# Rotary embedding and attention scores on one core: loads that follow a store issued as 64-row halves, with four loads through GpSimd in place of five

## The chip, the core and the metric

The kernel runs on one core of a Trainium2 chip. Its engines are TensorE (PE, matrix products; its weight loads are shown apart as PEld), VectorE (DVE), ScalarE (ACT), GpSimd (POOL) and SyncE (SP). Work of different engines is ordered by semaphores. Data moves between the core's on-chip memory (SBUF, 128 partitions) and the device's memory through 16 DMA engines. SyncE and GpSimd issue these transfers on rings of their own, and a transfer that an engine issues is spread over several or all of the 16. TensorE writes its results to PSUM, from where ScalarE or VectorE copies them to SBUF.

The metric is the time of one execution in device microseconds (us). Smaller is better.

## What is computed

Queries and keys get a rotary embedding, then each query row is multiplied with all key rows of its batch and head:

```python
batch, seq, heads, dim = 16, 512, 16, 64
q1, q2 = q[..., :half_dim], q[..., half_dim:]
q_rot = concatenate([q1 * cos - q2 * sin, q1 * sin + q2 * cos], axis=-1)
# k_rot the same from k
scores = einsum('bshd,bthd->bsht', q_rot, k_rot)
```

All is float32. The inputs q and k have 33.6 MB each, the output 16 x 512 x 16 x 512 values or 268.4 MB. The output is by far the most of the traffic.

## The kernel before

**Tiles and steps.** A batch has 512 rows. They are laid out so that SBUF partition p holds rows 4p to 4p+3; such a quarter, 128 rows with one of the four offsets, is a chunk (C = 4 chunks a batch). The kernel makes 64 steps, one for each chunk of q (`i` from 0 to 63, batch `i // 4`). In a step, TensorE forms the scores of 128 query rows against all 512 key rows, two heads at a time (`scores(i, p)` for p from 0 to 7), ScalarE copies each pair of heads from PSUM to the staging tile (line 418), and after the last pair the staging tile, 128 x 8192 values or 4 MB, is stored with one DMA (line 426). There are three staging tiles (`st`), used in turn; a tile may be filled again when its store has landed. The first batch is done in another order and stores 16 pieces of 1 MB.

**Preparing the chunks.** VectorE applies the rotary embedding in place (line 335), TensorE transposes the chunk through a small PSUM bank (line 360), and VectorE or ScalarE copies it to `qT` or `kT` (line 378). Within a step, the next chunk of q and a chunk of the next batch's k are prepared between the score products.

**Loads.** A batch of q or of k is 2 MB, 16 KB on each of the 128 partitions, and is loaded whole into one of two buffers for each of q and k (`load`, line 264). In the third step of a batch q of the batch after next is loaded, in the fourth step k of the batch after that (lines 507 to 510). SyncE issues them in the same ring as the stores, in the order in which the program's list has them: the store of the step, then the load.

**Loads around one DMA engine.** The kernel takes it that DMA engine 4 works more slowly than the other 15 (`SLOW = 4`). Five loads of q, those of batches 5, 8, 11, 13 and 15 (`RELIEVED`, line 260), are therefore split. [...] 

**Waits.** `Plan.add` records every operation with the keys that it reads and writes, and `Plan.resolve` works out from the keys which semaphore each has to await. A DMA names its own semaphore, for example `out0` for the first staging tile. A load's two groups of keys, `rows` and `rest`, let its two parts be awaited together where they come by different transfers. Line numbers of DMAs in the profile are those of the helper that records them (line 237).

Of the kernel before, what the change touches and what calls it, by code (L numbers as in the profile page):

```python
# [7 lines left out]
PE, ACT, DVE, POOL, SP = "PE", "ACT", "DVE", "POOL", "SP"  # L8
# [170 lines left out]
def kernel(  # L179
# [8 lines left out]
    nc = tc.nc  # L188
# [4 lines left out]
    B, S, H, D = q.shape  # L193
    HD = D // 2
    P = 128
    C = S // P
    HP = H // 2
# [8 lines left out]
    dram = {  # L206
        "q": q.rearrange("b (p c) h d -> b p c h d", c=C),
        "k": k.rearrange("b (p c) h d -> b p c h d", c=C),
    }
    o_v = out.rearrange("b (p c) h t -> b c p h t", c=C)  # L210
# [18 lines left out]
    def one(f):  # L229
        def emit():  # L230
            a = f()
            return a, a

        return emit

    def dma(engine, e, dst, src, sem, reads=(), writes=(), also=()):
        plan.add(engine, one(lambda: e.dma_start(dst, src)), reads, writes, sem=sem, also=also)  # L237
# [19 lines left out]
            writes=[("unit", which, u) for u in us], also=[x for u in us for x in unit_keys(which, u)],  # L257
        )

    RELIEVED = {("q", 5): 0, ("q", 8): 1, ("q", 11): 2, ("q", 13): 3, ("q", 15): 4}  # L260
    tiny = [0]
    SLOW = 4

    def load(which, b):
        if b >= B:
            return
        t = inb[which][b % 2]
        sem = f"in_{which}{b % 2}"
        rows = [("in", which, b % 2, c) for c in range(C)]
        rest = [("in rest", which, b % 2, c) for c in range(C)]  # L270
        if (which, b) not in RELIEVED:
            dma(SP, nc.sync, t.rearrange("p c (h d) -> p c h d", h=H), dram[which][b], sem, writes=rows + rest)
            return

        n, E, F = 120, C * H * D, C * H * D // 2
        x = RELIEVED[which, b]
        d = dram[which][b]  # L280

        def move_cursor(k):
            y = tiny[0]
            tiny[0] += 1
            src = bass.AP(q.tensor, 512 * y, [(512, k), (64, 2), (1, 2)])
            dst = scratch[:k, 4 * y : 4 * y + 4].rearrange("p (a b) -> p a b", a=2)
            dma(POOL, nc.gpsimd, dst, src, "cursor", writes=[("scratch", y)])

        def halves(lo, hi, keys, sem):
            src = bass.AP(d.tensor, d.offset + lo * E + F, [(E, hi - lo), (-F, 2), (1, F)])  # L290
            v = t[lo:hi]
            dst = bass.AP(v.tensor, v.offset + F, [(v.ap[0][0], hi - lo), (-F, 2), (1, F)])
            dma(POOL, nc.gpsimd, dst, src, sem, writes=keys)

        plan.add(POOL, None, (), rows)
        if x % 2:
            move_cursor(8)
            halves(n, P, rest, f"rest{x}")
        move_cursor(SLOW + 1)
        halves(0, n, rows, f"part{x}")  # L300
        if not x % 2:
            dma(SP, nc.sync, t[n:].rearrange("p c (h d) -> p c h d", h=H), d[n:], sem, writes=rest)
# [9 lines left out]
    def rope(which, n):  # L312
        if n < C:
            x = units[which, n]
            sv, k1, k2 = "p c (g j) -> p c g j", {"j": HD}, {"j": D}
            cs = cos_t.unsqueeze(2).to_broadcast((P, C, 2 * G, HD))
            ss = ss_v.unsqueeze(2).to_broadcast((P, C, G, D))
            pv = part.rearrange("p (c g j) -> p c g j", c=C, j=D)
            x5 = x.rearrange("p c (h x j) -> p c h x j", x=2, j=HD)
            p5 = part.rearrange("p (c h x j) -> p c h x j", c=C, x=2, j=HD)  # L320
            adds = [(x5[:, :, :, y], p5[:, :, :, 1 - y]) for y in range(2)]
        else:
            x = inb[which][n // C % 2][:, n % C]
            sv, k1, k2 = "p (g j) -> p g j", {"j": HD}, {"j": D}
            cs = cos_t[:, n % C].unsqueeze(1).to_broadcast((P, 2 * H, HD))
            ss = ss_v[:, n % C].unsqueeze(1).to_broadcast((P, H, D))
            pv = part.rearrange(sv, **k2)
            x4 = x.rearrange("p (h x j) -> p h x j", x=2, j=HD)
            swapped = bass.AP(part.tensor, part.offset + HD, [part.ap[0], (D, H), (-HD, 2), (1, HD)])
            adds = [(x4, swapped)]  # L330
        xs, xc = x.rearrange(sv, **k2), x.rearrange(sv, **k1)
        keys, more = src_keys(which, n), src_also(which, n)

        def tt(o, a, b, op, reads, writes):
            plan.add(DVE, one(lambda: nc.vector.tensor_tensor(o, a, b, op=op)), reads, writes, also=more)  # L335

        def products():
            tt(pv, xs, ss, mult, keys + ["ss"], ["part"])
            tt(xc, xc, cs, mult, keys + ["cos"], keys)

        def sums():
            for y, z in adds:
                tt(y, y, z, add, keys + ["part"], keys)

        return [products, sums]
# [34 lines left out]
    def stage_of(i):  # L380
        return i % 2 if i < C else (i - 2) % NST_BUFS
# [4 lines left out]
    def ps_of(i, p):  # L386
        m = HP * i + p if i < FIRST else HP * ((i - FIRST) % PERIOD) + p
        if i >= FIRST and m >= HP * PERIOD - 3:
            return (1, 2, 1)[m - (HP * PERIOD - 3)]
        return m % NPS  # L390

    def scores(i, p):
        y, s = ps_of(i, p), stage_of(i)
        ps, st = ps_s[y], stage[s]
        b = i // C
        if b == 0:
            c, hp = divmod(p, 2)
            lhs, rhs = qTb[i % 2][:, C * hp + c], kTb[0][:, 2 * i + hp]
            keys = [("qT", i % 2, C * hp + c)] + [("kT", 0, 2 * i + hp, x) for x in range(C)]
        else:  # L400
            lhs, rhs = qTb[i % 2][:, p], kTb[b % 2][:, p]
            keys = [("qT", i % 2, p)] + [("kT", b % 2, p, x) for x in range(C)]

        def emit():
            done = []
            for r in range(2):
                lo, hi = 64 * r, 64 * r + 64
                done.append(
                    nc.tensor.matmul(out=ps[:, r, :], lhsT=lhs[lo:hi, :], rhs=rhs[lo:hi, :], start=True, stop=True)  # L409
                )  # L410
            return done[0], done[-1]

        plan.add(PE, emit, keys, [("ps", y)])
        so, si = st[:, 2 * p : 2 * p + 2, :], ps
        if b > 0:
            so = so.rearrange("s r (t c) -> s r t c", c=C)
            si = si.rearrange("s r (c t) -> s r t c", c=C)
        plan.add(ACT, one(lambda: nc.scalar.copy(out=so, in_=si)), [("ps", y)], [("st", s, p)])  # L418
        if b == 0 and p % 2 == 1:
            c = p // 2  # L420
            dma(
                SP, nc.sync, o_v[0, c, :, G * i : G * (i + 1)], st[:, G * c : G * (c + 1)], f"out{s}_{c}",
                reads=[("st", s, p - 1), ("st", s, p)],
            )
        elif b > 0 and p == HP - 1:
            dma(SP, nc.sync, o_v[b, i % C], st, f"out{s}", reads=[("st", s, x) for x in range(HP)])

    def tr_act(which, n):
        for g in range(2):
# [2 lines left out]
    def run(ops):  # L432
        for op in ops:
            op()
# [3 lines left out]
    for head, heads in ((0, G), (G, H - G)):  # L438
        load_units("k", head, heads)
        load_units("q", head, heads)  # L440
    load("k", 1)
    load("q", 1)
    plan.add(POOL, one(lambda: nc.gpsimd.memset(ident, 0.0)), (), ["ident"])
    plan.add(
# [3 lines left out]
                out=ident, in_=ident, compare_op=mybir.AluOpType.not_equal, fill=1.0, base=0,  # L448
# [11 lines left out]
    for i in range(C):  # L460
        plan.step = i
        if i < C - 1:
            dve = rope("k", i + 1) + rope("q", i + 1) + rope("k", C + i)
            nxt = [("k", i + 1), ("q", i + 1)]
        else:
            dve = rope("q", C) + rope("k", C + i) + rope("q", C + 1) + rope("k", 2 * C)
            nxt = [("q", C), ("k", C + i)]
# [16 lines left out]
    for i in range(C, NST):  # L484
        plan.step = i
        tr = {}
        if i + 1 < NST:
            tr[1], tr[3] = ("q", i + 1, 0), ("q", i + 1, 1)
        if i + C < NST:
            tr[5], tr[6] = ("k", i + C, 0), ("k", i + C, 1)  # L490
        dve = []
        if i + 2 < NST:
            dve += rope("q", i + 2)
        if i + 1 + C < NST:
            dve += rope("k", i + 1 + C)
        for p in range(HP):
            scores(i, p)
            if p not in tr:
                continue
            if tr[p][0] == "q":  # L500
                run(dve[:1])
                dve = dve[1:]
                transposed(*tr[p], DVE)
            else:
                transposed(*tr[p], ACT)
        run(dve)
        if i % C == C - 2:
            load("q", i // C + 2)
        elif i % C == C - 1:
            load("k", i // C + 3)  # L510

    plan.resolve()
    with tc.tile_critical(), nc.cleanup_on_exit():
# [33 lines left out]
```

## Time and profile before

| | |
|---|---|
| Median of 3 runs | 797.21 us (795.77 to 797.94) |
| The profiled execution: its time | 797.94 us |
| its span in the profile | 796.2 us |
| PE matmuls, busy | 683.7 us (86%) |
| ACT, busy | 562.4 us (71%) |
| DVE, busy | 545.2 us (68%) |
| POOL, busy | 9.8 us (1%) |
| Moved by DMA | 335.87 MB, 422 GB/s over the span |
| Read from and written to device memory | 67.24 MB and 268.44 MB |

The page gives each engine's busy time, then a table in which the span is cut into 40 equal slices: a digit is the busy share of a slice in tenths, and the row GB/s says what the DMA engines moved. Below it stand the DMA queues, the chain of work that ended last, the costliest groups of instructions with the idle time before them, and the DMA issues with the median time from issue to landing. Two more views are used: the waits (who waited for whom: total, times, longest), and stretches of the span with the busy time of each engine (PE, PEld, DVE, ACT, POOL, each with its number of instructions), the clock granted to TensorE, the DMA engines' share and their rate. The trace also keeps a record of every DMA packet (start, duration, size, ring) and of every step by which a transfer counted up its semaphore, one for each DMA engine that took part.

### The profile page before, as it was taken

To read this page: it belongs to the slowest core of one execution; us is meant where nothing else is said; L and a number is where in the kernel's file an instruction comes from. 1 tells how busy PE (TensorE), PEld (TensorE's weight loads), DVE (VectorE), ACT (ScalarE), POOL (GpSimd) and SP (SyncE) were. 2 spreads that over 40 slices of the span, in tenths; PEclk is the share of its full clock that TensorE was granted. 3 is DMA by queue.
4 is the path that set the end of the run, shared out by engine and by line. 5 is a ranking of instruction groups with operands and counts; after the bars stand their busy time and mean duration, and the time that the engine had idled before them with its cause. 6 is when DMAs were issued, how large, how long until landed. Compare 5 with 4: busy or idle time off the path is not lost.

```text
span 796.2 us, 8200 instructions
## 1 busy us (share of the span) xinstructions
PE 683.7 (86%) x3072; PEld 294.7 (37%) x3072; DVE 545.2 (68%) x516; ACT 562.4 (71%) x647; POOL 9.8 (1%) x20
## 2 busy tenths in 40 slices
PE   3989999896998979899797988979978899799960
PEld 2444444342433434334342433334433344344420
DVE  6999988585785868658586767667756678576400
ACT  2978887684866858578585866767857777589760
POOL 0000000000000000100000000000100000000000
PEclk9999999897998989989899999999999999899995
DMA  8999999999999999999999999999999999999996
GB/s 347 419 425 437 423 394 435 425 436 423 435 417 428 435 433 424 433 424 411 432 426 439 430 433 427 429 424 428 435 428 419 421 440 427 429 433 431 434 430 278
DMA packets 18689, 335.87 MB, mean 422 GB/s; under 512 B 2184, under 2 KB 3464, under 8 KB 4488
## 3 DMA queue, kind: packets, MB, share of 16 engines
q1 hardware_dynamic: 16704, 325.46, 96.1%
q0 software_dynamic: 1680, 10.10, 3.0%
q10 hardware_dynamic: 288, 0.13, 0.1%
q8 instruction: 6, 0.10, 0.0%
q14 instruction: 11, 0.09, 0.0%
HBM read 67.24 MB, written 268.44 MB: 422 GB/s over the span
## 4 chain that ended last, share of the span: by engine, by line
DMA 47%; PE 35%; DVE 8%; ACT 6%; issue 1%; ACTq 0%; DVEq 0%; SPq 0%
DMA out_dram<-st 47%; PE ps L409 27%; PE bank L360 9%; ACT st L418 5%; DVE st L335 3%; DVE part L335 2%; DVE k_sb L335 2%; DVE q_sb L335 1%; DMA sin_t<-in_sin_dram 1%; DVE kT L378 0%; DVE qT L378 0%; ACTq L237 0%; ACT ss_t L455 0%; ACT ss_t L454 0%; ACTq L110 0%
## 5 line engine op out<-in xcount | busy, mean ns | idle before, releaser
L418 ACT COPY st<-ps 128x1024 f32<-128x1024 f32 x512 | 495.5, 1019 | 194.6 <-DMA out_dram<-st 108.5
L409 PE MATMUL ps<-kT,qT 64*128 64x512 f32 x2048 | 542.3, 645 | 70.2 <-ACT st L418 70.2
L409 PEld LDWEIGHTS ps<-kT,qT 64*128 64x128 f32 x2048 | 181.4, 194 | 259.8 <-issue 129.9
L378 DVE COPY qT<-bank 128x512 f32<-128x512 f32 x118 | 81.5, 691 | 195.5 <-PE bank L360 195.5
L360 PEld LDWEIGHTS bank<-ident,q_sb 128*128 128x128 f32 x480 | 54.6, 150 | 101.5 <-issue 98.8
L360 PE MATMUL bank<-ident,q_sb 128*128 128x128 f32 x480 | 85.5, 305 | 1.0 <-DVE q_sb L335 1.0
L360 PEld LDWEIGHTS bank<-ident,k_sb 128*128 128x128 f32 x480 | 50.5, 141 | 94.2 <-DVE k_sb L335 45.9
L360 PE MATMUL bank<-ident,k_sb 128*128 128x128 f32 x480 | 78.7, 287 | 1.6 <-DVE k_sb L335 0.8
L378 ACT COPY kT<-bank 128x512 f32<-128x512 f32 x122 | 72.6, 598 | 6.7 <-PE bank L360 6.7
L335 DVE TENSOR_TENSOR part<-q_sb,ss_t 128x1024 f32<-128x1024 f32 x60 | 73.5, 1225 | 3.2
L335 DVE TENSOR_TENSOR q_sb<-q_sb,cos_t 128x1024 f32<-128x1024 f32 x60 | 73.5, 1225 | 2.1
L335 DVE TENSOR_TENSOR k_sb<-k_sb,cos_t 128x1024 f32<-128x1024 f32 x60 | 73.5, 1225 | 2.0
L335 DVE TENSOR_TENSOR k_sb<-k_sb,part 128x1024 f32<-128x1024 f32 x60 | 73.5, 1225 | 2.1
L335 DVE TENSOR_TENSOR part<-k_sb,ss_t 128x1024 f32<-128x1024 f32 x60 | 72.9, 1215 | 0.3
L335 DVE TENSOR_TENSOR q_sb<-q_sb,part 128x1024 f32<-128x1024 f32 x60 | 72.9, 1215 | 0.0
L360 PE MATMUL bank<-ident,st 128*128 128x128 f32 x64 | 10.8, 318 | 14.3 <-DVE st L335 14.3
L360 PEld LDWEIGHTS bank<-ident,st 128*128 128x128 f32 x64 | 8.2, 161 | 19.6 <-DVE st L335 17.8
L335 DVE TENSOR_TENSOR part<-st,ss_t 128x1024 f32<-128x1024 f32 x8 | 9.8, 1223 | 7.4 <-ACT ss_t L455 7.0
L237 POOL DMA_DIRECT2D scratch<-in_q_dram x7 | 4.2, 598 | 661.5 <-PE bank L360 661.5
L335 DVE TENSOR_TENSOR st<-st,part 128x512 f32<-128x512 f32 x16 | 11.0, 690 | 0.5
L335 DVE TENSOR_TENSOR st<-st,cos_t 128x1024 f32<-128x1024 f32 x8 | 9.8, 1225 | 0.3
L378 ACT COPY qT<-bank 128x512 f32<-128x512 f32 x10 | 5.7, 618 | 3.5 <-PE bank L360 3.5
(11 smaller groups left out, 11.8 us busy)
## 6 DMA issues: line engine op xcount, KB each, us to landing
out_dram<-st SPq DMA_DIRECT2D x60, 4096.0 KB, 25.0
k_sb<-in_k_dram SPq DMA_DIRECT2D x15, 2048.0 KB, 27.0
q_sb<-in_q_dram SPq DMA_DIRECT2D x10, 2048.0 KB, 29.3
out_dram<-st SPq DMA_DIRECT2D x16, 1024.0 KB, 12.9
q_sb<-in_q_dram POOLq DMA_DIRECT2D x5, 1920.0 KB, 29.8
st<-in_k_dram SPq DMA_DIRECT2D x1, 1536.0 KB, 9.6
st<-in_q_dram SPq DMA_DIRECT2D x1, 1536.0 KB, 12.8
st<-in_k_dram SPq DMA_DIRECT2D x1, 512.0 KB, 5.7
```

What stands on the lines that cost most here:

```text
L237: plan.add(engine, one(lambda: e.dma_start(dst, src)), reads, writes, sem=sem, also=also)
L335: plan.add(DVE, one(lambda: nc.vector.tensor_tensor(o, a, b, op=op)), reads, writes, also=more)
L360: done = [nc.tensor.transpose(bank[:, x, :], srcs[x], ident) for x in range(4)]
L378: plan.add(engine, one(lambda: copy(out=dst, in_=src)), [("bank", m)], keys)
L409: nc.tensor.matmul(out=ps[:, r, :], lhsT=lhs[lo:hi, :], rhs=rhs[lo:hi, :], start=True, stop=True)
L418: plan.add(ACT, one(lambda: nc.scalar.copy(out=so, in_=si)), [("ps", y)], [("st", s, p)])
```

## The change

A load that follows a store on SyncE's ring is now recorded together with that store, inside `scores`: the store of rows 0 to 63, the load of rows 0 to 63, the store of rows 64 to 127, the load of rows 64 to 127. The second halves have semaphores of their own (`out0_64`, `in_q0_64` and so on). `load_behind(i)` says which load follows the store of step i; the two lines at the end of a step that called `load` are gone. A store that no load follows, or one followed by a load that goes by GpSimd, stays whole. The first loads, ahead of step 4, stay whole too. So 21 pairs of a store and a load are split: the loads of q for batches 3, 4, 6, 7, 9, 10, 12, 13 and 15, and the loads of k for batches 4 to 15.

The loads of q that go around engine 4 are now those of batches 5, 8, 11 and 14, where they were 5, 8, 11, 13 and 15. Batch 14's has the form of the loads of batches 8 and 13, with the last eight rows by GpSimd.

```diff
-    RELIEVED = {("q", 5): 0, ("q", 8): 1, ("q", 11): 2, ("q", 13): 3, ("q", 15): 4}
+    RELIEVED = {("q", 5): 0, ("q", 8): 1, ("q", 11): 2, ("q", 14): 3}
...
-    def load(which, b):
+    def load_behind(i):
+        if i % C == C - 2 and i // C + 2 < B:
+            return "q", i // C + 2
+        if i % C == C - 1 and i // C + 3 < B:
+            return "k", i // C + 3
+        return None
+
+    def load(which, b, part_rows=None):
...
         if (which, b) not in RELIEVED:
-            dma(SP, nc.sync, t.rearrange("p c (h d) -> p c h d", h=H), dram[which][b], sem, writes=rows + rest)
+
+            lo, hi = part_rows or (0, P)
+            keys = {0: rows + rest if hi == P else rows, 64: rest}[lo]
+            dma(
+                SP, nc.sync, t[lo:hi].rearrange("p c (h d) -> p c h d", h=H), dram[which][b][lo:hi],
+                sem if lo == 0 else f"{sem}_{lo}", writes=keys,
+            )
             return
...
         elif b > 0 and p == HP - 1:
-            dma(SP, nc.sync, o_v[b, i % C], st, f"out{s}", reads=[("st", s, x) for x in range(HP)])
+            keys, nxt = [("st", s, x) for x in range(HP)], load_behind(i)
+            if nxt is None or nxt in RELIEVED:
+                dma(SP, nc.sync, o_v[b, i % C], st, f"out{s}", reads=keys)
+                if nxt is not None:
+                    load(*nxt)
+                return
+
+            for lo in (0, 64):
+                hi = lo + 64
+                dma(SP, nc.sync, o_v[b, i % C][lo:hi], st[lo:hi], f"out{s}" + "_64" * (lo > 0), reads=keys)
+                load(*nxt, (lo, hi))
...
         run(dve)
-        if i % C == C - 2:
-            load("q", i // C + 2)
-        elif i % C == C - 1:
-            load("k", i // C + 3)
```

## The prediction

> **What bounds the kernel now.** I read the table of slices first, to see whether one resource is full throughout. The last slice ends the span, so its 6 is the tail, not a gap.
>
> ```profile
> DMA  8999999999999999999999999999999999999996
> GB/s 347 419 425 437 423 394 435 425 436 423 435 417 428 435 433 424 433 424 411 432 426 439 430 433 427 429 424 428 435 428 419 421 440 427 429 433 431 434 430 278
> ```
>
> The 16 DMA engines are busy nine tenths or more in all slices but the first and last, and what varies is only the rate. The queues come next: nearly all of it is SyncE's ring (q1), and GpSimd's ring (q0) carries the five loads that go around engine 4.
>
> ```profile
> q1 hardware_dynamic: 16704, 325.46, 96.1%
> q0 software_dynamic: 1680, 10.10, 3.0%
> ```
>
> Then the waits and the issues, to see whether the ring ever runs short.
>
> ```profile
> SPq L237 <- ACT st L418: 712.9, 75, 18.2
> ```
>
> ```profile
> out_dram<-st SPq DMA_DIRECT2D x60, 4096.0 KB, 25.0
> k_sb<-in_k_dram SPq DMA_DIRECT2D x15, 2048.0 KB, 27.0
> ```
>
> SyncE waits for ACT nearly always, yet a 4 MB store lands 25.0 us after its issue although its own packets need 8 x 1.21 = 9.7 us on each engine. So about 15 us of earlier work stands in the ring whenever something is added: engines PE, DVE and ACT have that much cover, and the time is the time in which the slowest DMA engine works off its share.
>
> What is lost against a full rate is read from stretches: two without a GpSimd load, then three with one (the columns end with DMA share and GB/s).
>
> ```profile
> 416.00:476.00 60.00, 51.84 (x230) 22.01 (x232) 40.44 (x39) 42.24 (x49) 0.00 (x0) 0.94 1.00 432
> 526.00:569.00 43.00, 38.44 (x172) 16.20 (x168) 30.40 (x30) 29.46 (x35) 0.00 (x0) 0.92 1.00 432
> 324.00:375.00 51.00, 46.05 (x194) 19.52 (x196) 33.61 (x32) 37.10 (x43) 2.48 (x4) 0.90 1.00 418
> 471.00:521.00 50.00, 43.33 (x190) 18.68 (x192) 32.89 (x32) 35.72 (x41) 1.33 (x2) 0.93 1.00 425
> 569.00:620.00 51.00, 42.87 (x190) 18.18 (x188) 33.38 (x31) 36.02 (x42) 2.48 (x4) 0.93 1.00 423
> ```
>
> Quiet stretches run at 432 GB/s whether they hold loads or not, so a load behind a store costs nothing as such. A GpSimd load costs the mean engine 51 x 14/432 = 1.7, 0.8 and 1.1 us.
>
> Below the views lie the trace's packet and completion records. A 32 KB store packet took 1213 ns at the median and at the 90th percentile, a 16 KB load packet 611 ns; the time above that sums to 2.8 us an engine for these stores and 5.3 us for the loads. In every quiet stretch one engine alone is slow: about three quarters of its store packets take 1236 to 1265 ns, so it falls back 0.25 to 0.33 us a store. I take it for engine 4, the one that the GpSimd loads spare. At the end the 16 engines finish within 6.4 us: the slow one last, 4.9 us after the median, another 0.2 us ahead of it, a third 1.2 us ahead.
>
> **The change, part by part.** Base of the sum: the profiled execution, 797.94 us (span 796.2), which is 0.73 above the median of three.
>
> *One GpSimd load fewer.* By bytes, a spared load takes 8 x 611 ns = 4.9 us off the slow engine. Its lag shows less. Around the first four, four stores and two loads would take it 4 x 9.68 + 2 x 4.86 + 1.3 of drift = 49.7 us; its completions lie 48.9, 49.1, 48.2 and 48.4 us apart, a gain of 0.8, 0.6, 1.5 and 1.3. Around the last (three stores and one load, 34.8) it took 32.3: a gain of 2.5. The rest went into its own stores: in the first window ten of its packets took 1.44 to 1.59 us. The change drops batch 13 (two tiny cursor transfers, an 8-row and a 120-row load on GpSimd; gain 1.3) and batch 15 (one cursor transfer and 120 rows there, eight rows on SyncE; 2.5); both come back on SyncE as split loads. Batch 14 leaves SyncE and takes the form of 8 and 13 (0.6 and 1.3, so 1.0). Sum for the slow engine: 1.3 + 2.5 - 1.0 = +2.8 us. Bounds: +0.6, the smallest gain seen, and +4.9, all bytes. The other engines save some 1 us, but the slow one ends the run.
>
> *42 more DMAs.* 21 pairs are split (nine loads of q, twelve of k). Each added DMA adds one count-up packet of 9 ns per engine: 42 x 9 = 0.4 us. On SyncE a store issue takes 0.33 us and a load issue 0.9 to 1.0, so 1.3 us more per pair, hidden in the 15 us of ring; without that cover it would be 21 x 1.3 = 27 us. ACT and DVE wait on one more semaphore 21 times each; the producers are the same transfers, so only their order counts.
>
> *The order in a pair.* The second store half stands behind half a load: it lands 4 x 611 = 2.4 us later, and ACT's first copy into that buffer with it; behind that copy on ACT stand the evictions that free PSUM, which PE awaits (70.2 us in all). The load ends when it did. 2.4 us comes out of 15 us: nothing; uncovered it would be 21 x 2.4 = 51 us. The loads were already behind the store in the plan, with the same readers to await, and move past no other store.
>
> *The 64-row form* is not in the trace, and is the open price: 168 store and 168 load packets per engine. Nearest rows: the eight-row loads on SyncE's ring, which also give an engine fewer rows of few partitions: of 24 packets 22 took 611 ns, two 1047 and 727, a mean of +23 ns. GpSimd's 120-row loads: 8 KB packets at a mean of 309.8 ns against 309. Against that, the loads before pay a mean of 28 ns a packet already. So: nothing. Upper bound: every packet as in the worst full load (768 ns, +157) and in the slow engine's worst window (1470, +257): 168 x 0.414 = 70 us. Lower bound: the halves end the loads' excess (-5.3 us) and halve the slow rows on the slow engine in 21 stores (168 x 0.75 x 40 ns / 2 = -2.5 us).
>
> [...]
>
> Sum: 797.94 + 2.8 + 0.4 + 0 = 801.1 against the profiled execution; from the median, 800.4. I forecast 801.
>
> **Rivals.** What a measurement of this kernel can tell from no change is 0.3%, 2.4 us.
>
> *The slowness belongs to rows, not to the engine.* Then a half hands half of the slow partitions to another engine: -2.5, so 798.6, less 0.7 from the median: 798, no change. For: only stores are slow, never loads. Against: no row shows any other engine slow.
>
> *Faster: the finer mixing keeps engines in step.* Loads lose 5.3 us an engine, nearly all in six of them (means of 652 to 768 ns), four of these the first after a GpSimd load, while settled ones run at 611 to 614. If halves stay settled: 801.1 - 5.3 - 2.5 = 793.3. For: there is one disturbance fewer. Against: two row patterns per pair are more to settle, not fewer.
>
> *Slower, the halves unsettle every pair.* The four unsettled loads after GpSimd loads paid 8 x 54 to 127 ns, mean 0.7 us; at 21 loads +15, so 816; with the stores of the pair hit as well up to 871 (the 70 us). It decides as soon as split loads average above 640 ns.
>
> [...]
>
> **How the numbers follow.** Forecast 801 (799.6 to 806): 0.40. Rows: 0.15. Faster: 0.12. Unsettled halves, 806 to 871: 0.22. Far slower: 0.11. So faster 0.12, same 0.15, slower 0.40 + 0.22 + 0.11 = 0.73. Range 793 to 840: from the faster rival up into the unsettled one; left out are the far case, the unsettled one's top (some 0.05) and a little below 793. The likeliest case's own range is 798.5 (+0.6) to 803.2 (+4.9 with the 0.4), so 798 to 804.
>
> **What would show it.** Right: quiet stretches with split pairs at 430 GB/s or more, split packets at 1213 and 611 ns, the slow engine alone last and 6 us or more behind the median. Rows: a final lag below 5 us. Unsettled: split stretches below 425 GB/s. [...] Cover gone: DMA digits below 9. The forecast is wrong if a split packet's price is not near zero, which the trace bounds but doesn't show.

## The result and the profile after

The changed kernel takes 979.25 us (median of 6 runs, 965.44 to 989.55) against 797.09 us before: a ratio of 1.219 (95% interval 1.212 to 1.226), slower by 182 us by the medians and by 175 us by the ratio. The profiled execution took 975.93 us with a span of 974.2. Executions of the kernels below whose 64-row transfers are slow scatter by 1 to 7%, those of the others by 1.3% at most; a ratio counts only the executions within 1.5% of their kernel's fastest (here 965.44 to 975.93), and of the slow kernels only differences beyond their scatter are read.

The table of slices of the changed kernel, its DMA share and its rate:

```profile
DMA  9999999999999989999999999999989999799996
GB/s 359 410 424 438 270 322 357 346 343 356 310 360 320 334 221 299 374 398 342 382 393 351 287 317 419 303 363 282 341 296 307 363 408 304 290 254 425 428 432 265
```

The first four slices are nearly as before. From the fifth on, where the first pair is split, the rate is 221 to 419 GB/s, and it is back at 425 to 432 in slices 37 to 39, where no load is left to split. The DMA engines are nearly as busy as before all the while: in the first split pair below a share of 0.99 goes with 251 GB/s, so busy says that a packet is under way, not that it moves at full speed.

Stretches of the changed kernel around the first split pair (the last two columns are DMA share and GB/s):

```profile
60.00:97.00 37.00, 35.96 (x174) 15.66 (x170) 35.99 (x33) 31.76 (x38) 0.00 (x0) 1.00 1.02 433
97.00:109.00 12.00, 12.00 (x60) 5.54 (x60) 9.88 (x11) 10.15 (x13) 0.00 (x0) 1.00 0.99 251
109.00:115.00 6.00, 6.00 (x32) 2.58 (x30) 5.22 (x6) 5.33 (x7) 0.00 (x0) 1.00 0.98 273
```

Within one pair the rate falls from 433 to 251 GB/s at a share of 0.99. The packet records say how. Between 100 and 107 us, in the middle of the first split pair, 26 of 49 packets of 32 KB took 2500 to 2600 ns, most of them 2547 to 2551, twice the 1213 of before; of the 64 load packets between 97 and 115 us 12 took 611 ns as before and 24 took 1239 to 1310. Over the whole run 62 store packets took 4.7 us and more.

The costliest groups, first of the kernel before, then of the changed one (behind the first bar busy us and mean ns of one, behind the second the idle us before it and what ended most of them):

```profile
L409 PE MATMUL ps<-kT,qT 64*128 64x512 f32 x2048 | 542.3, 645 | 70.2 <-ACT st L418 70.2
L418 ACT COPY st<-ps 128x1024 f32<-128x1024 f32 x512 | 495.5, 1019 | 194.6 <-DMA out_dram<-st 108.5
```

```profile
L422 PE MATMUL ps<-kT,qT 64*128 64x512 f32 x2048 | 569.2, 670 | 215.5 <-ACT st L431 215.5
L431 ACT COPY st<-ps 128x1024 f32<-128x1024 f32 x512 | 496.5, 1019 | 371.9 <-DMA out_dram<-st 273.7
```

The changed kernel's DMA issues (count, KB each, median us to landing):

```profile
out_dram<-st SPq DMA_DIRECT2D x39, 4096.0 KB, 34.7
out_dram<-st SPq DMA_DIRECT2D x42, 2048.0 KB, 26.3
k_sb<-in_k_dram SPq DMA_DIRECT2D x24, 1024.0 KB, 31.8
```

ACT's copies cost the same (495.5 us before, 496.5 now), but wait 273.7 us for stores, 2.5 times the former 108.5, and PE waits for ACT 215.5 us, formerly 70.2. A whole store lands 34.7 us after its issue, formerly 25.0. The engines are held by the ring, not the other way round.

Summed over the packet records and taken as a mean over the 16 DMA engines, packets took 938.9 us of the span of 974.2 (790.4 of 796.2 before), so an engine stood idle for 35.3 us (5.7 before). Of the 178 us between the two spans 148 are longer packets and 30 idle time.

### The profile page after: what moved, and what is told of

The parts are those of the page before. It is cut to its first block, busy times and chain, and to the rows that moved or that the text cites. A ratio compares the mean times of both kernels' runs of the same rounds, so it can differ in the third digit from the quotient of the medians.

```text
span 974.2 us, 8239 instructions
## 1 busy us (share of the span) xinstructions
PE 717.0 (74%) x3072; PEld 304.1 (31%) x3072; DVE 545.2 (56%) x516; ACT 563.4 (58%) x647; POOL 8.4 (1%) x18
## 4 chain that ended last, share of the span: by engine, by line
DMA 61%; PE 24%; DVE 5%; ACT 5%; SPq 3%; issue 1%; ACTq 0%; DVEq 0%
DMA out_dram<-st 60%; PE ps L422 18%; PE bank L373 6%; ACT st L431 5%; SPq L237 3%; DVE part L348 1%; DVE st L348 1%; DVE k_sb L348 1%; DVE q_sb L348 1%; DMA st<-in_k_dram 1%; DVE kT L391 0%; DVE qT L391 0%; ACTq L110 0%; DVEq L110 0%; SPq L561 0%
## 5 line engine op out<-in xcount | busy, mean ns | idle before, releaser
L422 PE MATMUL ps<-kT,qT 64*128 64x512 f32 x2048 | 569.2, 670 | 215.5 <-ACT st L431 215.5
L431 ACT COPY st<-ps 128x1024 f32<-128x1024 f32 x512 | 496.5, 1019 | 371.9 <-DMA out_dram<-st 273.7
L422 PEld LDWEIGHTS ps<-kT,qT 64*128 64x128 f32 x2048 | 186.5, 202 | 417.8 <-ACT st L431 281.4
L373 PEld LDWEIGHTS bank<-ident,q_sb 128*128 128x128 f32 x480 | 58.9, 159 | 111.6 <-issue 105.0
L373 PE MATMUL bank<-ident,q_sb 128*128 128x128 f32 x480 | 92.0, 322 | 1.0 <-DVE q_sb L348 1.0
## 6 DMA issues: line engine op xcount, KB each, us to landing
out_dram<-st SPq DMA_DIRECT2D x39, 4096.0 KB, 34.7
```

Of the source, the lines that this page charges most:

```text
L373: done = [nc.tensor.transpose(bank[:, x, :], srcs[x], ident) for x in range(4)]
```

## The experiments

Theory A: which partitions a transfer has is what costs the time, 64 adjacent ones from 0 or from 64. By it a kernel whose halves have other partitions runs near 797 us, and one whose halves have these near 979. What makes such a transfer slow no run shows. Its rivals were the order and number of the transfers, the addresses in device memory, 64 rows as such, and the missing fifth GpSimd load. Unless it says otherwise, each diff is against the changed kernel; the kernel before, on the same chip, took 797.1 to 797.2 us.

**Cut by columns instead of rows.**

```diff
-                dma(SP, nc.sync, o_v[b, i % C][lo:hi], st[lo:hi], f"out{s}" + "_64" * (lo > 0), reads=keys)
+                h0, h1 = lo // 8, hi // 8
+                dma(
+                    SP, nc.sync, o_v[b, i % C][:, h0:h1], st[:, h0:h1], f"out{s}" + "_64" * (lo > 0),
+                    reads=[("st", s, x) for x in range(h0 // 2, h1 // 2)],
+                )
```

with `load` cut into chunks 0, 1 and 2, 3 in the same way.

> The changed kernel with its pairs cut by columns in place of rows: store of heads 0 to 7 on all 128 partitions, load of chunks 0 and 1 on all 128, store of heads 8 to 15, load of chunks 2 and 3. Order, number of DMAs, semaphores and the four GpSimd loads are the changed kernel's; each packet is half as long (16 KB and 8 KB), with as many more. [...] Rival B (the alternation of store and load halves, or the 42 added DMAs, cost the time whatever the partitions): 960 to 990 us.

Measured: 804.0 us, ratio 1.0094 (1.0078 to 1.0109). The same order, the same 42 added DMAs, but all partitions in each: 175 us are gone. One thing more differs: the first store half awaits only the copies of its own heads, and a chunk only its own half of the load; the kernel with every second partition, below, keeps the changed kernel's waits. Order and count are not the cause; some 5 us over the kernel with four GpSimd loads remain theirs, or the shorter packets'.

**Four GpSimd loads and nothing cut.**

```diff
-    RELIEVED = {("q", 5): 0, ("q", 8): 1, ("q", 11): 2, ("q", 13): 3, ("q", 15): 4}
+    RELIEVED = {("q", 5): 0, ("q", 8): 1, ("q", 11): 2, ("q", 14): 3}
```

(against the kernel before)

> The kernel before with the four GpSimd loads of the changed one (batches 5, 8, 11 and 14) and nothing cut. My prediction's term for this part was +2.8 us with bounds +0.6 and +4.9: 797.7 to 802 us. Rival (the missing relief is what costs the time, because a late engine holds up all others): well above 810 us.

Measured: 798.84 us, ratio 1.0022 (1.0012 to 1.0031), so +1.0 to +2.5 us. The engines finish over 7.7 us, 6.4 before, the last one 5.2 us after the median, 4.9 before.

**Halves with five GpSimd loads.** The same line, the other way round.

> The changed kernel with the five GpSimd loads of the one before, so pairs cut into 64-row halves (20 of them) and nothing else changed. Theory A: within 10 us of the changed kernel, 965 to 990 us, since one relief is worth a few us. Rival (relief and halves act together: a late engine 4 makes the halves collide): 20 us or more below the changed kernel.

Measured: 967.6 us (961.0 to 971.3), ratio 1.216 (1.213 to 1.218). That is 12 us below the changed kernel by the medians and 3 by the ratios, within the scatter, where one pair fewer is worth 180/21 = 9 and the fifth load 1.6. The missing relief is not the cause.

**Every second partition.**

```diff
+                pick = slice(lo // 64, P, 2)
-                dma(SP, nc.sync, o_v[b, i % C][lo:hi], st[lo:hi], f"out{s}" + "_64" * (lo > 0), reads=keys)
+                dma(SP, nc.sync, o_v[b, i % C][pick], st[pick], f"out{s}" + "_64" * (lo > 0), reads=keys)
```

and the loads likewise.

> The changed kernel with halves of 64 rows that are every second partition: even rows first, then odd rows. Packets, their sizes, order and DMAs are the changed kernel's; each half now spans all 128 partitions. Theory A in its simple form (what counts is which partitions the transfer as a whole reaches): 797 to 810 us. [...] Rivals that blame the order, the number of DMAs or 64 rows as such: 960 to 990 us.

Measured: 804.2 us (800.0 to 810.4), ratio 1.0090 (1.0054 to 1.0126). Sixty-four rows as such cost at most the 5 us over the four-load kernel's 798.8. The slices of this kernel:

```profile
GB/s 339 422 426 431 435 390 439 427 436 430 414 431 426 418 431 421 421 431 410 432 421 432 415 432 420 411 435 424 434 412 427 427 418 416 426 436 430 434 428 265
```

No inner slice is below 390. The theory in its simple form, 797 to 810 us, fits. How the rows of such a transfer are dealt to the engines no run shows.

**Only the stores cut, and only the loads.** An estimate for both: if each packet of a cut transfer took twice its time ("in step"), as 26 of 49 store packets did above, a pair would lose 8 x 1.213 = 9.7 us on its store and 8 x 0.611 = 4.9 us on its load. Over 21 pairs that is 21 x 14.6 = 306 us, of which the changed kernel paid 180: this is its share. For the stores alone it makes 21 x 9.7 x 180/306, some 120 us over the four-load kernel, so 880 to 960 us with a margin of 40.

```diff
                 dma(SP, nc.sync, o_v[b, i % C][lo:hi], st[lo:hi], f"out{s}" + "_64" * (lo > 0), reads=keys)
-                load(*nxt, (lo, hi))
+            load(*nxt)
```

> The changed kernel with only its stores cut (rows 0 to 63, rows 64 to 127, then the load whole). [...]

```diff
+            dma(SP, nc.sync, o_v[b, i % C], st, f"out{s}", reads=keys)
             for lo in (0, 64):
-                hi = lo + 64
-                dma(SP, nc.sync, o_v[b, i % C][lo:hi], st[lo:hi], f"out{s}" + "_64" * (lo > 0), reads=keys)
-                load(*nxt, (lo, hi))
+                load(*nxt, (lo, lo + 64))
```

> The changed kernel with only its loads cut (store whole, then the load's rows 0 to 63 and 64 to 127). Theory A: in step +4.9 us a pair, +102 over 21, with the changed kernel's share some +60: 830 to 890 us. [...]

Measured: stores alone 980.5 us (967.4 to 1037.4, profiled 970.8), above the estimate and no less than the changed kernel; loads alone 855.2 us (841.6 to 863.7), as expected. So halves cost time in both directions, as stores and as loads. But the losses do not add: 182 and 56 over the four-load kernel (169 and 44 between the fastest executions) do not make the changed kernel's 180 (167). The packet records show the exchange. The time above 1213 ns (32 KB packets of stores) and 611 ns (16 KB packets of loads on SyncE's ring) is, as a mean over the DMA engines:

| cut | store packets | load packets |
|---|---|---|
| nothing (the kernel before) | 2.8 us | 5.3 us |
| stores | 132.5 us | 16.5 us |
| loads | 5.5 us | 47.2 us |
| both in turn (the changed kernel) | 96.1 us | 56.4 us |

With load halves in between, the store packets lose 36 us less and the load packets 40 us more.

**Other rows in device memory.**

```diff
-                dma(SP, nc.sync, o_v[b, i % C][lo:hi], st[lo:hi], f"out{s}" + "_64" * (lo > 0), reads=keys)
+                dma(SP, nc.sync, o_v[b, i % C][lo // 64 : P : 2], st[lo:hi], f"out{s}" + "_64" * (lo > 0), reads=keys)
```

and the loads likewise.

> The changed kernel's halves of 64 adjacent partitions, but on the side of device memory each half takes every second row of its chunk (even rows, then odd rows), as in the kernel with every second partition. So queries, keys and scores are moved to other rows within a batch: the result is permuted, the work is the same. Theory A (partitions count): 960 to 990 us. Rival (the addresses in device memory count, and every second row is what brought that kernel to 804): 797 to 810 us.

Measured: 982.2 us, ratio 1.229 (1.219 would be the changed kernel's). The device memory's rows are those of the kernel with every second partition, the partitions those of the changed one, and the time goes with the partitions.

**The second halves on ScalarE's ring.** The second ring was to have both halves of a transfer under way at once, so that the packets are not all on the same 64 partitions.

```diff
-                dma(SP, nc.sync, o_v[b, i % C][lo:hi], st[lo:hi], f"out{s}" + "_64" * (lo > 0), reads=keys)
+                dma(*((SP, nc.sync) if lo == 0 else (ACT, nc.scalar)), o_v[b, i % C][lo:hi], st[lo:hi], f"out{s}" + "_64" * (lo > 0), reads=keys)
```

and the loads likewise.

> The changed kernel's halves, with the second store half and the second load half issued by ScalarE on its own ring. [...] Theory A: most of the loss goes, 800 to 860 us; ScalarE pays some 2 us of issue a pair out of its idle time. Rival (a transfer of 64 adjacent partitions is slow on each engine whatever the others do): 950 us or more.

Measured: 936.9 us (924.4 to 946.3). Both sides missed. Only 42 us come back with ScalarE issuing the second halves (the 21 of the stores at a median of 0.51 us), and 138 us over the four-load kernel stay lost. Why is not shown: the packet records do not name the engine.

**Both store halves, then both load halves.**

```diff
                 dma(SP, nc.sync, o_v[b, i % C][lo:hi], st[lo:hi], f"out{s}" + "_64" * (lo > 0), reads=keys)
+            for lo in (0, 64):
-                load(*nxt, (lo, hi))
+                load(*nxt, (lo, lo + 64))
```

> The changed kernel's four 64-row transfers of a pair in another order: both store halves, then both load halves, so no alternation. [...] Rival (the order in the pair does not matter): 965 to 990 us, as the changed kernel.

Measured: 997.9 us (965.0 to 1007.9), scattered from the 965 to 990 us of an order that does not matter up into the 1000 to 1060 us that were put for losses that add (the stores-only kernel's 182 us and the loads-only kernel's 56 us over 798.8, some 1035): one execution, 965.0, is as fast as the changed kernel's fastest, three took 990 to 1008. Whether the alternation saves anything stays open.

**The middle partitions.** Against the stores-only kernel:

```diff
-                dma(SP, nc.sync, o_v[b, i % C][lo:hi], st[lo:hi], f"out{s}" + "_64" * (lo > 0), reads=keys)
+                dma(SP, nc.sync, o_v[b, i % C][lo:hi], st[32:96], f"out{s}" + "_64" * (lo > 0), reads=keys)
```

> The stores-only kernel, but both halves of a cut store read the staging tile's partitions 32 to 95, into rows 0 to 63 and rows 64 to 127 of the output chunk; loads whole. So in these 21 stores the scores of partitions 0 to 31 and 96 to 127 are not stored and others stand twice; the packets, bytes and order are the same. [...] Rival (64 adjacent partitions are slow wherever they begin, or 64-row stores as such): 960 to 1000 us, as the stores-only kernel's 980.

Measured: 799.8 us, ratio 1.0032 (1.0021 to 1.0043), against the stores-only kernel's 980. This is the sharpest pair of runs: 64 adjacent partitions in both, the same packets to the same rows of device memory, only 32 to 95 in place of 0 to 63 and 64 to 127. The slices of the stores-only kernel, then of this one:

```profile
GB/s 357 412 422 437 256 310 384 317 357 404 312 384 332 388 310 322 282 313 329 364 314 382 321 327 336 271 347 321 319 396 338 359 399 293 397 332 351 365 433 269
```

```profile
GB/s 346 416 423 431 436 418 427 428 429 427 426 416 425 427 436 425 433 427 422 427 426 439 424 438 424 423 422 427 435 427 434 436 431 417 422 439 429 437 427 247
```

256 to 433 GB/s become 416 to 439 in the same 35 slices, from the fifth to the 39th. So 64 adjacent partitions as such are not slow: in these stores those from 0 and from 64 are, and those from 32 are not. Why, no run shows.

**By columns, not alternating; and by columns with five GpSimd loads.** The first is the reordering above, applied to the kernel cut by columns; the second changes the line of the GpSimd loads.

> The kernel cut by columns (804.0 us), in the order both store halves, then both load halves. The 5 us that it has over the four-load kernel's 798.8 come either from the alternation of stores and loads (then this one falls to 798 to 800) or from the pieces themselves, 42 more DMAs and shorter packets (then it stays at 803 to 805).

> The kernel cut by columns with the five GpSimd loads of the one before: the change without its partitions and without its missing fifth load. [...]

Measured: 800.7 us, ratio 1.0046 (1.0032 to 1.0059), and 800.0 us, ratio 1.0046 (1.0030 to 1.0062), where 804.0 less the fifth load's 1.6 makes 802.4. Of the 5 us that the alternating columns have over the four-load kernel, the alternation costs 3.3 (804.0 - 800.7) and the pieces 1.9 (800.7 - 798.8). With the kernel before's own five loads, alternating columns are still slower than it by 0.3 to 0.6%, some 2.9 us; pieces and alternation would make 5.2, so the two prices hold for four loads and do not carry over as a sum. Alternating halves gain nothing even where each has all partitions, and no version here beats the kernel before.

## Why the prediction failed

**The step that failed is "the 64-row form ... So: nothing", and with it the upper bound of 70 us.** It is worth some 170 to 180 us. The nearest row misled in a plain way: an eight-row load is eight packets of 0.6 us, and of those the fourth in flight was already stretched by 436 ns. I took 22 undisturbed packets of 24 for a mean price, where the form asked about keeps the 16 engines on half of the partitions for a whole half transfer, at the packet times before 4 x 1.21 = 4.8 us a store and 4 x 0.61 = 2.4 us a load. Three packets that overlap for 0.3 us do not bound a sustained overlap; why short ones pass unharmed was not tested. The bound from "worst windows" was no bound either: it came from transfers over all 128 partitions. The trace of the kernel before has no row with 16 engines on 64 partitions, so nothing in it excluded a high price: the far slower case, which had a chance of 0.11 and was left out of the range, is what came. What that chance rested on no run shows; the runs showed 979.25 us against 797.09. The slowness holds for the halves 0 to 63 and 64 to 127, not for any 64 adjacent partitions, as the middle ones show (799.8 us). Its signs were a rate of 221 to 419 GB/s in the slices with split pairs, where the lowest inner slice before had 394, with a DMA share near 1, and ACT's wait on stores at 2.5 times 108.5 us.

**Twice the time for every split packet would have been too much.** So 168 store packets of 1.213 us and 168 load packets of 0.611 would lose 204 and 103 us. Above the kernel before's excess, the packets lost 93 and 51, about half. The engines drift apart: the 16 engines' completions of one transfer lie more than 25 us apart in seven places, where they lie 7.9 apart at most in the kernel before. That the drift is what lowers the loss was not tested. Against it stand 30 us more of idle time for each DMA engine, which the cover of 15 us in the ring, taken as enough in the prediction, did not prevent.

**What bounds the kernel** was read rightly: the DMA engines, with everything else behind 15 us of ring.

**One GpSimd load fewer**: the size fits, +2.8 us was forecast and +1.6 measured (1.0 to 2.5), inside the bounds of 0.6 and 4.9. That it comes from the slow engine's lag is not shown: in the profiled execution of the four-load kernel the last engine came 5.2 us after the median, 4.9 before, where 6 or more was expected; but that execution, 798.0 us, is the fastest of the eleven.

**42 more DMAs, 0.4 us, and the order in a pair, nothing**: too low with four loads, by columns 1.9 us for the pieces and 3.3 for the alternation. The pieces include packets of half the length there; 42 store halves of full packets on partitions 32 to 95, 21 DMAs more, make 1.0 us (799.8 - 798.8), which the two intervals do not tell from nothing.

**Rows own the slowness**, the rival of no change, was not put to a test. **Faster through finer mixing** did not come with the columns and five loads (800.0 us against 797.1); their pieces cost something too, so a gain smaller than that price is not excluded. **Unsettled halves** can be worth no more than the 3 to 5 us that alternating columns and every second partition cost.

## What to carry to other kernels

Before cutting a transfer by partitions, ask which partitions each piece has, not how many: in these runs pieces of 0 to 63 and 64 to 127 fell to little more than half the rate (251 against 433 GB/s in the first pair), while stores of 32 to 95, and stores and loads of every second partition, ran at nearly the full rate (inner slices of 416 and 390 GB/s or more). If a transfer must be cut, cut it along the free dimension or by stride (804.0 and 804.2 us here, against 979.25); no cut here beat the whole transfer (797.1). A DMA engine's busy share does not show it (0.99 at 251 GB/s): read GB/s and the duration of single packets. And where the nearest row of the trace is of another kind, widen the bound until the missing kind fits in.

## What the runs showed that was not expected

Many packets of the first split pairs took twice the time and 5% more (2550 ns against 1213, 1290 against 611), and 62 of the run's 7680 store packets of 32 KB took 4.7 us and over, about four times as long. What stretches them by such steps no run shows.

The issue itself slowed down. SyncE's store issues took at most 0.86 us before and up to 4.9 us in the changed kernel; a load of k took 1.03 us at the median before, 2.6 in the stores-only kernel and 0.85 with the middle partitions. SyncE (SPq) was then 3% of the chain of work that ended last, where it had been 0%; first the kernel before, then the changed one:

```profile
DMA 47%; PE 35%; DVE 8%; ACT 6%; issue 1%; ACTq 0%; DVEq 0%; SPq 0%
```

```profile
DMA 61%; PE 24%; DVE 5%; ACT 5%; SPq 3%; issue 1%; ACTq 0%; DVEq 0%
```

So SyncE, which feeds the slow ring, was itself held up, by up to 4.9 us in one issue, and with it whatever it would issue next. What makes the issues longer, a full ring or something else, was not tested.
